# A hybrid layer on one core: the recurrent projection's products placed by unit, keys stored twice, two recurrent pools swapped

## The chip, the cores and the metric

One core of one Trainium2 chip runs the whole layer as one program. The metric is the device time of an execution in microseconds, given as the median of three runs. The engines are named as in the profile: PE (TensorE, matmuls), DVE (VectorE), ACT (ScalarE), POOL (GpSimd) and SP (SyncE, which here only issues DMAs). Sixteen DMA engines move data between HBM and the on-chip memory.

## The reference

One layer over 1024 latent and 256 context tokens, all in f32, 1024 channels:

```python
xn = modulate(rms_norm(x), sh1, sc1);  cn = modulate(rms_norm(h_ctx), csh1, csc1)
yg, xr, q, k, v, gr, gn = split_in(xn @ w_in[l] + b_in[l])     # seven parts of 1024
...                                                             # conv, gated linear recurrence, two directions
y_rnn = h_lat * jax.nn.gelu(yg)
q4 = axial_rope(q...);  k4 = axial_rope(k...)                   # 16 heads of 64
y_na = neighbourhood_attention(q4, k4, v4, kc4, vc4, na_rpb[l]) # window 8 x 16 plus 256 context keys
mix = jax.nn.sigmoid(gr) * (y_rnn @ w_proj_rnn[l]) + jax.nn.sigmoid(gn) * (y_na @ w_proj_na[l])
x = x + g1 * (mix @ w_out[l])
x = x + g2 * expert_choice_moe(xn2, w_router[l], w_exp_gate[l], w_exp_up[l], w_exp_down[l])  # 16 experts
return rms_norm(x) * final_norm
```

## The kernel before

Every f32 product is made of three products: an operand is split into a rounded high part and the rest (`hi`, `lo`), and `mm3` (lines 185 to 189) adds hi·hi, hi·lo and lo·hi in one PSUM tile. The stages follow each other: queries, keys and values (`stage_qkv`), the recurrent branch (`stage_lru`), attention (`stage_attn`), the merge of both branches, and the experts. No planner orders the instructions: each engine takes them in the order in which the Python code issues them, and waits in that order. SP's DMAs stand in one queue; each of them waits until the DMA that last used its semaphore, one of eight, has landed.

Weights come as chunks of 1 MB through `Stream`: `load` fetches a chunk into one of two ring tiles, `split` makes its `hi` on ACT (line 181) and its `lo` on DVE (line 98), and `take` hands it to PE, drops the one before and splits what has been loaded.

`stage_qkv` runs over four groups of four heads: query units, key units, value units, on PE some 80 us in all. A finished pair of units is rotated on DVE and POOL, then `out_parts` (line 477) splits it (`ohi` on ACT, `olo` on DVE, three buffers each) and stores both halves to HBM with line 484: four rows of 32 partitions by up to 512 tokens. Value results (`vo`, line 617, four buffers) are stored by line 618; in SP's queue these stores stand behind the group's key stores. `mod_rows` works on other weights (`wmr`, 16 MB through POOL's queue) beside this.

`stage_lru` weaves projections (PE) with a chain of elementwise work and scans (ACT, DVE, POOL) over eight blocks of 128 channels. It stores `y_rnn` as `d_yr` (line 752). Its tiles lie in the pools `tgp`, `lru2`, `lru3`, `lru1`, stacked in that order; the attention stage's pools come to lie over them, so a first load of the attention stage waits until whatever used those bytes is done.

`stage_attn` has 128 units n: a head and a strip of 128 queries. `attend` issues for unit n: `score` (products `sp`, then on DVE bias and row maximum, line 909), `turn` of unit n-3 (transposes `pt`, line 932, copied by ACT to `et`, line 934; `pt` has one buffer), `values` of units n-5 and n-6, `expo` (ACT), `scale` (DVE). `project` multiplies `y_rnn` by the weights `wpr`: two halves of 512 tokens, eight output blocks, eight groups (one `mm3` of three matmuls) per block. `weave` interleaves the two by a running cost that each yields:

```python
done += 0.55        # attend, after score; 0.5 after turn, 1.2 per two units for values
...
if k % 2 == 1:      # project: two groups at a time
    done += 0.8 * f
    yield done
```

The operand of these products, `y_rnn` as the tiles `x0h`, `x1h`, `x0l`, `x1l` of 1 MB each, is fetched by line 1012 for each half.

Of the kernel before, what the change touches and what calls it, by code (L numbers as in the profile page):

```python
# [12 lines left out]
F32 = mybir.dt.float32  # L13
F32R = mybir.dt.float32r
# [39 lines left out]

SKIP1, SKIP2 = 7, 7
IDLE = 1
A1, A2 = 3, 4

LRU_ORDER = ([("in", 0)] + [e for j in range(1, 6) for e in (("in", j), ("gate", j - 1))]
# [3 lines left out]
def raw(t, off, dims):  # L63
    return bass.AP(tensor=t.tensor, offset=t.offset + off, ap=dims)


class Stream:
# [33 lines left out]
    def split(self, most=9, defer=False, pieces=1):  # L101

        k = self.k
        most += self.nsplit
        while self.nsplit < min(self.nload, most) and self.chunks[self.nsplit][2] and self.pfree:
            i = self.nsplit
            slot = self.pfree.popleft()
            hi = slot[0].tile([128, 2048], F32R, name=slot[1] + "h", tag=slot[1] + "h")
            lo = slot[0].tile([128, 2048], F32R, name=slot[1] + "l", tag=slot[1] + "l")
            x, rslot = self.raws.pop(i)  # L110
            if pieces > 1:
                n = 2048 // pieces
# [12 lines left out]
            self.nsplit += 1  # L125

    def release(self):
        for i in self.held:
# [45 lines left out]
class Kernel:  # L174
# [28 lines left out]
    def run(self):  # L203
        tc, nc = self.tc, self.nc
        P = self.pools = {}
        left = []

        def open_(name, side="left", **kw):
            cm = tc.tile_pool(name=name, side=side, **kw)
            pool = cm.__enter__()  # L210
            return pool, cm

        self.open_ = open_
        self.const, c0 = open_("const", bufs=1)
        self.dram, c1 = open_("dram", bufs=1, space=DRAM)
        self.hip, c2 = open_("hip", bufs=1)
        self.ringp, c3 = open_("ringp", bufs=1)
        dr = lambda name, shape: self.dram.tile(shape, F32, name=name)
        self.d_q = self.dram.tile([16, 128, SEQ], F32R, name="d_q")
        self.d_k = self.dram.tile([16, 128, NT], F32R, name="d_k")  # L220
        self.d_v = dr("d_v", [10, 128, D])
        self.d_tgr = dr("d_tgr", [8, 128, SEQ])
        self.d_tgn = dr("d_tgn", [8, 128, SEQ])
        self.d_yr = [self.dram.tile([8, 128, SEQ], F32R, name="d_yr" + part) for part in "hl"]
        self.d_yn = [self.dram.tile([8, 128, SEQ], F32R, name="d_yn" + part) for part in "hl"]
        self.d_m1 = dr("d_m1", [8, 128, SEQ])
# [90 lines left out]
    def stage_qkv(self):  # L317
# [159 lines left out]
        def out_parts(dst, g, part, r, tok, n):  # L477
# [4 lines left out]
            width = dst.shape[2]  # L482
            for h, o in ((hi, 0), (lo, 64)):
                nc.sync.dma_start(raw(dst.bitcast(F32), (g * 512 + o + part * 32) * width + tok,
                                      [[128 * width, 4], [width, 32], [1, n]]), h[:, :n].bitcast(F32))

        def mod_rows():

# [166 lines left out]
    def stage_lru(self):  # L655
        nc, I, S = self.nc, self.I, self.S
        tgp, ctg = self.open_("tgp", side="right", bufs=1)
        p, cp = self.open_("lru2", side="right", bufs=1)
        last, clast = self.open_("lru3", side="right", bufs=1)
        first, cfirst = self.open_("lru1", side="right", bufs=1)  # L660
        ps, cps = self.open_("psl", bufs=1, space=PSUM)
        cneg, cpos = self.softplus_neg(first)
# [175 lines left out]
        weave(proj(), chain())  # L838
        cps.__exit__(None, None, None)
        cfirst.__exit__(None, None, None)  # L840
        clast.__exit__(None, None, None)
        cp.__exit__(None, None, None)
        ctg.__exit__(None, None, None)
        self.c_xn.__exit__(None, None, None)

# [2 lines left out]
    def stage_attn(self):  # L848
# [10 lines left out]
        def load_head(h):  # L859
# [5 lines left out]
            ks = []  # L865
            for part in range(2):
                t = pool.tile([128, NT], F32R, name=f"k{part}", tag=f"k{part}", bufs=2)
                for x in range(2):
                    nc.sync.dma_start(t[x * 64:(x + 1) * 64].bitcast(F32),
                                      self.d_k[h, part * 64:(part + 1) * 64].bitcast(F32))  # L870
                ks.append(t)
            L["h", h] = (q, ks)
        def load_v(h):
            if h < HEADS:
                v = (po if h % 4 else pb).tile([128, 10, 128], F32, name="v", tag="v")
# [83 lines left out]
                    nc.gpsimd.dma_start(d[pr, :, (s // 4) * 512:(s // 4 + 1) * 512].bitcast(F32), t.bitcast(F32))  # L959

        def attend():
            done = 0.0
            load_head(0)
            load_head(1)
            load_bias(0)
# [3 lines left out]
            for n in range(N + 6):  # L969
                if n < N:  # L970
# [17 lines left out]
                    done += 0.55  # L988
                if 0 <= n - 3 < N:
                    turn(n - 3)  # L990
                    done += 0.5
                if 0 <= n - 5 < N:
                    values(n - 5)
                    done += 1.2 * (n % 2 == 0)
                if n < N:
                    expo(n)
                yield done
                if 0 <= n - 1 < N:
                    scale(n - 1)

        def project():
            done = 5.0
            yield done
            f = 1.75

            def fetch(hf):

                ys = []
# [12 lines left out]
                    nc.sync.dma_start(tgs[hf, j], self.d_tgr[j, :, hf * 512:(hf + 1) * 512])  # L1021

            fetch_gate(0, 0)
            for hf in range(2):
                cs = slice(hf * 512, (hf + 1) * 512)
                yh, yl = fetch(hf)
                done += 12.0
                yield done
                for i in range(4):
                    hi, lo = S.take8()  # L1030
                    for x in range(2):
                        j = 2 * i + x
                        xs = slice(x * 128, (x + 1) * 128)
# [1 line left out]
                        fetch_gate(hf + (j + 1) // 8, (j + 1) % 8)  # L1035
                        pm = ps.tile([128, 512], F32, name="pr", tag="pr", bufs=1)
                        for k in range(8):
                            self.mm3(pm, hi[:, k, xs], lo[:, k, xs], yh[k // 4][:, k % 4], yl[k // 4][:, k % 4],
                                     k == 0, k == 7)
                            if k % 2 == 1:  # L1040
                                done += 0.8 * f
                                yield done
# [3 lines left out]
                        done += 2.0 * f  # L1046
                        yield done

        weave(attend(), project())
        cps.__exit__(None, None, None)  # L1050
        cpk.__exit__(None, None, None)
        cpo.__exit__(None, None, None)
# [920 lines left out]
```

## Time and profile before

| | |
|---|---|
| median of 3 runs | 2628.53 us (2625.5 to 2629.2) |
| profiled execution | 2631.97 us, its span on the core 2630.2 us |
| PE busy | 2490.4 us, 95% |
| DVE, ACT, POOL busy | 1888.0, 1535.5, 301.9 us |
| mean granted clock of PE | 0.978 of full speed |

The span is what lies between the first and the last instruction of the profiled execution. The queries, keys and values end at about 388 us, the recurrent stage at 844, attention at 1217; merge and experts take the rest. A busy share over the whole span hides that these stages have different limits, so windows of single stages are read below.

### The profile page before, as it was taken

Reading aid. Unit: us, or ns where it says so; the run is one execution under the profiler, and the core shown is the slowest. Engines: PE = TensorE matmul, PEld = TensorE weight load, DVE = VectorE, ACT = ScalarE, POOL = GpSimd, SP = SyncE. Lnnn points to the kernel's source line nnn. Section 1 sums busy time; section 2 is a strip of 40 time slices with the busy share of each in tenths; the row PEclk is TensorE's granted clock in tenths of the full one; section 3 lists DMA queues with packets and bytes.
Section 4 is the critical chain, followed back from the end, with each engine's and each line's share of the span. In section 5 each row is a group of like instructions: output and inputs, shape, how many; then the busy total and the mean of one; then the engine's idle time right before and its main releaser. Section 6 shows DMA issues by size and latency. Waiting matters only on the chain.

```text
span 2630.2 us, 34531 instructions
## 1 busy us (share of the span) xinstructions
PE 2490.4 (95%) x13401; PEld 2035.6 (77%) x13401; DVE 1888.0 (72%) x2300; ACT 1535.5 (58%) x1699; POOL 301.9 (11%) x269
## 2 busy tenths in 40 slices
PE   7999999999998799999997799999999999999996
PEld 4888888777886687787986577777777777777775
DVE  5675633655564566666466788888888898888888
ACT  5321125466655556565333577777777777777776
POOL 1321110121120000000120000000000000000001
PEclk9999999999999899999998899999999999999998
DMA  8354441122216959645875799999999999999985
GB/s 274 131 206 169 180 141 36 66 74 86 97 42 202 287 187 291 187 153 211 272 238 202 282 362 367 366 365 364 372 372 370 376 370 366 367 367 367 365 306 226
DMA packets 260148, 661.80 MB, mean 252 GB/s; under 512 B 18001, under 2 KB 35553, under 8 KB 250257
## 3 DMA queue, kind: packets, MB, share of 16 engines
q1 hardware_dynamic: 236768, 585.18, 62.8%
q0 software_dynamic: 15120, 62.21, 7.0%
q10 hardware_dynamic: 8096, 12.21, 1.5%
q8 instruction: 105, 1.72, 0.3%
q14 instruction: 59, 0.48, 0.1%
HBM read 585.02 MB, written 74.53 MB: 251 GB/s over the span
## 4 chain that ended last, share of the span: by engine, by line
PE 72%; DVE 10%; ACT 9%; DMA 5%; issue 3%; SPq 0%; ACTq 0%; POOLq 0%; DVEq 0%
PE pm L188 9%; PE pm L189 9%; PE pm L187 9%; PE po L187 3%; PE po L189 3%; PE po L188 3%; PE pv L949 2%; PE pp L187 2%; PE pp L188 2%; PE pp L189 2%; PE pt L932 2%; PE mm L187 2%; PE mm L189 2%; PE mm L188 2%; DVE w0l L98 2%
## 5 line engine op out<-in xcount | busy, mean ns | idle before, releaser
L98 DVE TENSOR_TENSOR w1l<-ring,w1h 128x2048 fp32r<-128x2048 f32 x150 | 343.3, 2288 | 72.5 <-ACT w1h L181 72.0
L98 DVE TENSOR_TENSOR w0l<-ring,w0h 128x2048 fp32r<-128x2048 f32 x123 | 281.8, 2291 | 81.6 <-ACT w0h L181 81.2
L181 ACT CAST w1h<-ring 128x2048 fp32r<-128x2048 f32 x150 | 286.2, 1908 | 70.8 <-PE pm L189 42.6
L181 ACT CAST w0h<-ring 128x2048 fp32r<-128x2048 f32 (+1 forms) x125 | 236.8, 1895 | 101.2 <-PE pm L189 45.2
L98 DVE TENSOR_TENSOR x0l<-ring,x0h 128x2048 fp32r<-128x2048 f32 x81 | 185.5, 2290 | 34.6 <-ACT x0h L181 34.4
L181 ACT CAST x0h<-ring 128x2048 fp32r<-128x2048 f32 x81 | 154.4, 1906 | 32.3 <-PE pm L189 16.3
L909 DVE CUSTOM_DVE_ANT_0 e<-sp,bias 128x640 f32<-128x640 f32 (+1 forms) x128 | 100.7, 787 | 83.1 <-PE sp L905 73.4
L188 PE MATMUL pm<-w0l,xeh 128*128 128x512 f32 x384 | 154.2, 402 | 2.8 <-DVE w0l L98 2.8
L187 PE MATMUL pm<-w0h,xeh 128*128 128x512 f32 x384 | 154.6, 403 | 1.7 <-ACT xeh L1681 1.7
L189 PE MATMUL pm<-w0h,xel 128*128 128x512 f32 x384 | 152.6, 397 | 0.0
L1760 POOL DMA_INDIRECT d_acc<-y,idx x15 | 50.5, 3366 | 873.0 <-DVE y L1759 873.0
L934 ACT COPY et<-pt 128x640 f32<-128x640 f32 (+1 forms) x128 | 84.7, 662 | 106.6 <-PE pt L932 104.9
L917 ACT ACTIVATE e<-e,mx 128x640 f32<-128x640 f32 (+1 forms) x128 | 103.0, 805 | 43.3 <-DVE mx L911 41.8
L187 PE MATMUL pm<-x0h,xeh 128*128 128x512 f32 x320 | 128.2, 401 | 0.0
L188 PE MATMUL pm<-w1l,xeh 128*128 128x512 f32 x320 | 128.1, 400 | 0.0
L187 PE MATMUL pm<-w1h,xeh 128*128 128x512 f32 x320 | 127.9, 400 | 0.0
L188 PE MATMUL pm<-x0l,xeh 128*128 128x512 f32 x320 | 126.8, 396 | 0.4 <-DVE x0l L98 0.4
L189 PE MATMUL pm<-w1h,xel 128*128 128x512 f32 x320 | 126.8, 396 | 0.0
L189 PE MATMUL pm<-x0h,xel 128*128 128x512 f32 x320 | 126.5, 395 | 0.0
L187 PE MATMUL pp<-xh,w1h 128*128 128x512 f32 (+1 forms) x304 | 116.3, 382 | 3.9 <-ACT tg L730 3.2
L188 PE MATMUL pp<-xl,w1h 128*128 128x512 f32 (+1 forms) x304 | 115.9, 381 | 0.0
L189 PE MATMUL pp<-xh,w1l 128*128 128x512 f32 (+1 forms) x304 | 115.7, 381 | 0.0
(458 smaller groups left out, 6894.0 us busy)
## 6 DMA issues: line engine op xcount, KB each, us to landing
ring<-w_exp_up SPq DMA_DIRECT2D x104, 1024.0 KB
ring<-w_exp_down SPq DMA_DIRECT2D x102, 1024.0 KB
ring<-w_exp_gate SPq DMA_DIRECT2D x100, 1024.0 KB
k<-d_k SPq DMA_DIRECT2D x64, 320.0 KB
wmr<-wm POOLq DMA_DIRECT2D x16, 1024.0 KB, 9.0
ring<-wrnn SPq DMA_DIRECT2D x16, 1024.0 KB
ring<-wqkv SPq DMA_DIRECT2D x12, 1024.0 KB
bias<-bias SPq DMA_DIRECT2D x16, 704.0 KB
```

The lines of the kernel that those rows point to most:

```text
L98: (engine or self.lo_engine).tensor_sub(lo, x, hi)
L181: self.nc.scalar.copy(hi, x)
L187: mm(out, wh, xh, start=first, stop=False)
L188: mm(out, wh, xl, start=False, stop=False)
L189: mm(out, wl, xh, start=False, stop=last)
L909: nc.vector.tensor_tensor_reduce(e[:, :w], sp[:, c0:c0 + w], b[:, b0:b0 + w], 1.0, -3.0e38, op0=ALU.add, op1=ALU.max, accum_out=mx[:, 0:1])
L917: nc.scalar.activation(e[:, :w], e[:, :w], AF.Exp, bias=mx[:, 1:2], accum_out=mx[:, 2:3])
L932: nc.tensor.transpose(pt[:, c * 128:(c + 1) * 128], e[:, c * 128:(c + 1) * 128], self.ident)
L934: nc.scalar.copy(et[:, :w], pt[:, :w])
L949: nc.tensor.matmul(pv[j * 64:(j + 1) * 64, (s % 4) * 128:(s % 4 + 1) * 128], v[:, t, j * 64:(j + 1) * 64], state[n - 1 + j][:, c * 128:(c ...
L1760: nc.gpsimd.indirect_dma_start(out=self.d_acc[:, :], out_offset=bass.IndirectOffsetOnAxis(ap=self.idx[:, e:e + 1], axis=0), in_=y[:, :], i ...
```

## The change

1. `out_parts` stores each half of a key twice, to rows 0 to 63 and 64 to 127 of a head's part, and `load_head` then reads 128 rows with one DMA where it read 64 rows twice.
2. `project` no longer yields a cost. It yields before each group, and `attend` yields after `score`: for unit n as many groups are issued there as the line through P0 and P1 (first half, 64 groups over 50 units from unit 11) and P2 and P3 (second half, 64 over 56 from unit 69) asks for. The fetch of the first half stands ahead of the unit loop's later loads; that of the second at the end of the first half.
3. `turn` comes four units behind (`BEHIND`) and not three, and after the products.
4. The next weight chunk is split in four pieces between products (`split_by`), not at once.
5. The pools `lru2` and `lru3` change places.

```diff
+BEHIND = 4
+P0, P1, P2, P3 = 11, 50, 69, 56
...
+    def split_by(self, n):
...
+        for c in range(0, 2048, 2048 // n):
+            cs = slice(c, c + 2048 // n)
+            self.k.hi_copy(hi[:, cs], x[:, cs])
+            self.lo_engine.tensor_sub(lo[:, cs], x[:, cs], hi[:, cs])
+            yield
...
-        self.d_k = self.dram.tile([16, 128, NT], F32R, name="d_k")
+        self.d_k = self.dram.tile([16, 2, 128, NT], F32R, name="d_k")
...
-            for h, o in ((hi, 0), (lo, 64)):
-                nc.sync.dma_start(raw(dst.bitcast(F32), (g * 512 + o + part * 32) * width + tok,
-                                      [[128 * width, 4], [width, 32], [1, n]]), h[:, :n].bitcast(F32))
+            step, at = (128, ((0,), (64,))) if dst is self.d_q else (256, ((0, 64), (128, 192)))
+            for h, os in zip((hi, lo), at):
+                for o in os:
+                    nc.sync.dma_start(raw(dst.bitcast(F32), (g * 4 * step + o + part * 32) * width + tok,
+                                          [[step * width, 4], [width, 32], [1, n]]), h[:, :n].bitcast(F32))
...
         tgp, ctg = self.open_("tgp", side="right", bufs=1)
+        last, clast = self.open_("lru3", side="right", bufs=1)
         p, cp = self.open_("lru2", side="right", bufs=1)
-        last, clast = self.open_("lru3", side="right", bufs=1)
...
-                for x in range(2):
-                    nc.sync.dma_start(t[x * 64:(x + 1) * 64].bitcast(F32),
-                                      self.d_k[h, part * 64:(part + 1) * 64].bitcast(F32))
+                nc.sync.dma_start(t.bitcast(F32), self.d_k[h, part].bitcast(F32))
...
-                if 0 <= n - 3 < N:
-                    turn(n - 3)
+                yield n
+                if 0 <= n - BEHIND < N:
+                    turn(n - BEHIND)
...
-                    hi, lo = S.take8()
+                    hi, lo = S.take8(most=0)
+                    more = S.split_by(4)
...
                         for k in range(8):
+                            yield
                             self.mm3(pm, hi[:, k, xs], lo[:, k, xs], yh[k // 4][:, k % 4], yl[k // 4][:, k % 4],
                                      k == 0, k == 7)
-                            if k % 2 == 1:
-                                done += 0.8 * f
-                                yield done
+                            if k % 4 == 2:
+                                next(more, None)
...
-        weave(attend(), project())
+        count, products = 0, project()
+        for n in attend():
+            if n == 0:
+                next(products)
+            due = min(64, (n - P0) * 64 // P1) + max(0, min(64, (n - P2) * 64 // P3))
+            while count < due:
+                next(products, None)
+                count += 1
+        for _ in products:
+            pass
```

SP's queue before, in the last group of the first stage: the key stores, the next weight chunk (`ring`), the value stores.

```order
L484 DMA d_k<-ohi 4x32x512
L484 DMA d_k<-olo 4x32x512
L484 DMA d_k<-ohi 4x32x512
L484 DMA d_k<-olo 4x32x512
L484 DMA d_k<-ohi 4x32x256
L484 DMA d_k<-olo 4x32x256
L484 DMA d_k<-ohi 4x32x256
L484 DMA d_k<-olo 4x32x256
L90 DMA ring_3098<-wrnn 128x2048
L618 DMA d_v<-vo 128x2x256 x5
```

The same place of SP's queue in the changed program, whose lines are numbered some 24 higher.

```order
L508 DMA d_k<-ohi 4x32x512 x2
L508 DMA d_k<-olo 4x32x512 x2
L508 DMA d_k<-ohi 4x32x512 x2
L508 DMA d_k<-olo 4x32x512 x2
L508 DMA d_k<-ohi 4x32x256 x2
L508 DMA d_k<-olo 4x32x256 x2
L508 DMA d_k<-ohi 4x32x256 x2
L508 DMA d_k<-olo 4x32x256 x2
L93 DMA ring_3146<-wrnn 128x2048
L642 DMA d_v<-vo 128x2x256 x5
```

Each key store has become two of the same shape, and weight chunk and value stores stand behind twice as many.

SP's queue before, at the start of attention, from the first pair's bias to the first two tiles of `y_rnn`.

```order
L882 DMA bias<-bias 128x1408 x2
L876 DMA v<-d_v 128x10x128
L864 DMA q<-d_q 128x1024
L869 DMA k_6452<-d_k 64x1280 x2
L869 DMA k_6455<-d_k 64x1280 x2
L882 DMA bias<-bias 128x1408 x2
L864 DMA q<-d_q 128x1024
L869 DMA k_6534<-d_k 64x1280 x2
L869 DMA k_6537<-d_k 64x1280 x2
L1021 DMA tgl<-d_tgr 128x512
L1012 DMA x0h<-d_yrh 128x4x512
L1012 DMA x1h<-d_yrh 128x4x512
```

The same place in the changed program.

```order
L905 DMA bias<-bias 128x1408 x2
L899 DMA v<-d_v 128x10x128
L1037 DMA tgl<-d_tgr 128x512
L1028 DMA x0h<-d_yrh 128x4x512
L1028 DMA x1h<-d_yrh 128x4x512
L1028 DMA x0l<-d_yrl 128x4x512
L1028 DMA x1l<-d_yrl 128x4x512
L93 DMA ring_6491<-wpr 128x2048
L1037 DMA tgl<-d_tgr 128x512
L888 DMA q<-d_q 128x1024
L892 DMA k_6511<-d_k 128x1280
L892 DMA k_6513<-d_k 128x1280
```

The tiles of `y_rnn` now stand ahead of the loads of the second pair of heads. The first bias load waited, before, for the last `hi` and `lo` stores of the recurrent stage and for its last gate stores; in the changed program for that `hi` store and for a subtraction before the `lo` store.

PE's order before, from the transposes issued with unit 13 over the first products to unit 14.

```order
L932 MATMUL pt<-ident,e 128x128 x5
L187 MATMUL pr<-x0h,w0h 128x512
L188 MATMUL pr<-x0l,w0h 128x512
L189 MATMUL pr<-x0h,w0l 128x512
L187 MATMUL pr<-x0h,w0h 128x512
L188 MATMUL pr<-x0l,w0h 128x512
L189 MATMUL pr<-x0h,w0l 128x512
L905 MATMUL sp<-k_6408,q 128x256
L905 MATMUL sp<-k_6411,q 128x256
L905 MATMUL sp<-k_6408,q 128x256
L905 MATMUL sp<-k_6411,q 128x256
L932 MATMUL pt<-ident,e 128x128 x5
```

The first products in the changed program, in unit 12.

```order
L928 MATMUL sp<-k_6456,q 128x256
L928 MATMUL sp<-k_6458,q 128x256
L928 MATMUL sp<-k_6456,q 128x384
L928 MATMUL sp<-k_6458,q 128x384
L208 MATMUL pr<-x0h,w0h 128x512
L209 MATMUL pr<-x0l,w0h 128x512
L210 MATMUL pr<-x0h,w0l 128x512
L955 MATMUL pt<-ident,e 128x128 x5
L972 MATMUL pv<-et,v 64x128 x10
```

The products moved from behind a unit's transposes to between its scores and the transposes, one group where two stood.

## Rows read from the trace of the kernel before

**Rows 1.** The page: busy time of PE, share of the span.
```profile
PE 2490.4 (95%) x13401; PEld 2035.6 (77%) x13401; DVE 1888.0 (72%) x2300; ACT 1535.5 (58%) x1699; POOL 301.9 (11%) x269
```
**Rows 2.** Stretches: length, busy us of each engine, PE's granted clock, DMA share, GB/s.
```profile
242.00:328.00 86.00, 86.00 (x510) 72.91 (x509) 57.83 (x91) 17.36 (x24) 15.12 (x14) 1.00 0.47 169
...
264.00:268.00 4.00, 4.00 (x19) 3.21 (x18) 3.88 (x6) 0.75 (x2) 0.97 (x1) 1.00 1.02 406
352.00:376.00 24.00, 24.00 (x196) 23.59 (x195) 6.93 (x9) 5.32 (x8) 3.09 (x2) 1.00 0.26 103
400.00:845.00 445.00, 433.12 (x1959) 353.74 (x1957) 248.42 (x178) 256.99 (x286) 72.68 (x65) 0.98 0.24 83
905.00:1150.00 245.00, 231.89 (x1857) 193.21 (x1858) 156.72 (x446) 141.62 (x269) 18.84 (x35) 1.00 0.73 225
1150.00:1217.00 67.00, 61.14 (x580) 50.71 (x579) 45.53 (x145) 45.67 (x90) 5.39 (x11) 1.00 0.40 131
```
**Rows 3.** The same for the start of attention, 845 to 905, with their sum.
```profile
850.00:860.00 10.00, 5.87 (x24) 4.89 (x24) 5.82 (x19) 4.25 (x10) 0.00 (x0) 0.53 1.07 305
...
880.00:890.00 10.00, 0.79 (x1) 0.28 (x1) 2.92 (x3) 1.94 (x3) 0.00 (x0) 0.50 0.98 348
...
sum 60.00, PE 38.95 PEld 31.68 DVE 29.66 ACT 27.04 POOL 1.63; mean PE 5.57 PEld 4.53 DVE 4.24 ACT 3.86 POOL 0.23
```
**Rows 4.** Who waited for the stores of line 484, 60 to 480: us, times.
```profile
  ACT ohi L479: 36.5, 8
  DVE olo L481: 34.8, 10
```
**Rows 5.** DMA from the first key store (86) to 392: total; issues, KB each.
```profile
DMA packets 19467, 51.60 MB, mean 169 GB/s; under 512 B 1075, under 2 KB 8243, under 8 KB 16067
...
d_k<-ohi SPq DMA_DIRECT2D x16, 256.0 KB
...
d_q<-ohi SPq DMA_DIRECT2D x14, 256.0 KB
...
d_k<-ohi SPq DMA_DIRECT2D x8, 128.0 KB
```
**Rows 6.** The chain that ended last, in the second group: start, us, what.
```profile
193.15 14.21 DMA d_k<-olo
...
210.08 0.60 DVE vo L617
```
**Rows 7.** Timeline, end of the third group and of the stage: start, us, instruction, idle before.
```profile
293.42 0.42 DVE L481 TENSOR_TENSOR olo<-qr,ohi 128x256 fp32r<-128x256 f32 x1 [4.71 <-DMA d_k<-olo]
...
314.63 0.69 DVE L617 TENSOR_TENSOR vo<-pv,bv 128x512 f32<-128x512 f32 x1 [3.83 <-DMA d_v<-vo]
...
389.05 0.36 PE L187 MATMUL pp<-xh,w0h 128*128 128x256 f32 x1 [0.88 <-DVE vo L617]
...
391.57 1.28 ACT L637 ACT_TABLE_LOAD   x1 [21.20 <-DMA d_v<-vo]
```
**Rows 8.** PE's timeline at its first two products: start, us, instruction, idle before.
```profile
884.96 0.79 PE L187 MATMUL pr<-x0h,w0h 128*128 128x512 f32 x1 [7.37 <-DMA x0h<-d_yrh]
890.35 0.79 PE L188 MATMUL pr<-x0l,w0h 128*128 128x512 f32 x1 [4.59 <-DMA x0l<-d_yrl]
```
**Rows 9.** Waits (DVE's, SP's; total, times, longest) and two of SP's issues, 845 to 870.
```profile
DVE e L909 <- DMA bias<-bias: 9.5, 2, 7.0
...
SPq L882 <- DMA d_yrl<-gel: 8.9, 1, 8.9
...
845.92 0.83 SPq L882 DMA_DIRECT2D bias<-bias  x2
...
868.80 0.38 SPq L1012 DMA_DIRECT2D x0h<-d_yrh  x1
```
**Rows 10.** What the transposes waited for from 905 to 1217: us, times.
```profile
  ACT et L934: 31.9, 63
  DVE e L924: 8.1, 9
```

More of the change, by code (lines that the diff above doesn't have):

```diff
@@ L125, in split @@
             self.nsplit += 1
+    def split_by(self, n):
+        i = self.nsplit
+        if i >= self.nload or not self.chunks[i][2] or not self.pfree:
+            return
+        self.nsplit += 1
+        slot = self.pfree.popleft()
+        hi = slot[0].tile([128, 2048], F32R, name=slot[1] + "h", tag=slot[1] + "h")
+        lo = slot[0].tile([128, 2048], F32R, name=slot[1] + "l", tag=slot[1] + "l")
+        x, rslot = self.raws.pop(i)
+        for c in range(0, 2048, 2048 // n):
[3 more added lines that the diff above has]
+            yield
+        self.free.append(rslot)
+        self.parts[i] = (hi, lo, slot)
     def release(self):
@@ L481, in out_parts @@
             nc.vector.tensor_sub(lo[:, :n], r[:, :n], hi[:, :n])
-            width = dst.shape[2]
-            for h, o in ((hi, 0), (lo, 64)):
-                nc.sync.dma_start(raw(dst.bitcast(F32), (g * 512 + o + part * 32) * width + tok,
-                                      [[128 * width, 4], [width, 32], [1, n]]), h[:, :n].bitcast(F32))
+            width = dst.shape[-1]
+            step, at = (128, ((0,), (64,))) if dst is self.d_q else (256, ((0, 64), (128, 192)))
[3 more added lines that the diff above has]
+                                          [[step * width, 4], [width, 32], [1, n]]), h[:, :n].bitcast(F32))
         def mod_rows():
@@ L840, in stage_lru @@
         cfirst.__exit__(None, None, None)
+        cp.__exit__(None, None, None)
         clast.__exit__(None, None, None)
-        cp.__exit__(None, None, None)
         ctg.__exit__(None, None, None)
@@ L961, in attend @@
         def attend():
-            done = 0.0
             load_head(0)
@@ L987, in attend @@
                     score(n)
-                    done += 0.55
-                if 0 <= n - 3 < N:
-                    turn(n - 3)
-                    done += 0.5
+                yield n
+                if 0 <= n - BEHIND < N:
+                    turn(n - BEHIND)
                 if 0 <= n - 5 < N:
                     values(n - 5)
-                    done += 1.2 * (n % 2 == 0)
                 if n < N:
                     expo(n)
-                yield done
                 if 0 <= n - 1 < N:
@@ L1001, in project @@
         def project():
-            done = 5.0
-            yield done
-            f = 1.75
             def fetch(hf):
@@ L1023, in project @@
             fetch_gate(0, 0)
+            yh, yl = fetch(0)
             for hf in range(2):
                 cs = slice(hf * 512, (hf + 1) * 512)
-                yh, yl = fetch(hf)
-                done += 12.0
-                yield done
                 for i in range(4):
-                    hi, lo = S.take8()
+                    hi, lo = S.take8(most=0)
+                    more = S.split_by(4)
                     for x in range(2):
@@ L1037, in project @@
                         for k in range(8):
+                            yield
                             self.mm3(pm, hi[:, k, xs], lo[:, k, xs], yh[k // 4][:, k % 4], yl[k // 4][:, k % 4],
                                      k == 0, k == 7)
-                            if k % 2 == 1:
-                                done += 0.8 * f
-                                yield done
+                            if k % 4 == 2:
+                                next(more, None)
                         m = po.tile([128, 512], F32, name="m1", tag="m1", bufs=2)
@@ L1045, in project @@
                         nc.gpsimd.dma_start(self.d_m1[j, :, cs], m)
-                        done += 2.0 * f
-                        yield done
-        weave(attend(), project())
+                    for _ in more:
+                        pass
+                if hf == 0:
+                    yh, yl = fetch(1)
+                yield
+        count, products = 0, project()
[7 more added lines that the diff above has]
+        for _ in products:
+            pass
         cps.__exit__(None, None, None)
```

## The prediction

> **What bounds the kernel now.** The busy table comes first: PE is busy for 95% of the span [rows 1], so a change is worth what it takes from or adds to PE's idle time. The stretches by stage show where that lies [rows 2]. In the query/key/value stage PE has no gap in the third group (86.00 of 86.00 us), in the recurrent stage it is busy 433.12 of 445. In attention it is busy 38.95 of the first 60 us [rows 3], then 231.89 of 245 and 61.14 of 67: 21.0, 13.1 and 5.9 us idle, 40 in all. [...]
>
> The DMA columns of the same rows tell of the stage whose stores are doubled. From 352 to 376 almost only key stores move: share 0.26, 103 GB/s. From 264 to 268 loads move as well: share 1.02, 406 GB/s. So a key store occupies some four of the sixteen engines, and several of them in the queue go no faster than one. ACT and DVE already wait 36.5 and 34.8 us for the stores' buffers [rows 4], and in the second group the chain that ended last runs for 14.21 us through a key store, to the `vo` behind it [rows 6].
>
> **The doubled key stores.** There are 16 of 256 KB and 8 of 128 KB for the high halves, as many for the low ones: 10.49 MB [rows 5]. At 103 GB/s [rows 2] that is 102 us of those four engines; the change adds 102 more. Is there room? The first key store is issued at about 86 us, and at 391.57 [rows 7] ACT enters the recurrent stage when the value stores have landed: 306 us. In them the core moves 51.60 MB [rows 5]. Key stores and 28 query stores (14 high and as many low, 256 KB each, 7.34 MB) are 17.8 MB on four engines, 173 us; the other 33.8 MB use all of them, at 406 GB/s 83 us. That is 256 of 306, 50 us free. The added 102 overrun this by 52 us, if not a microsecond of the four engines stays unused.
>
> How PE comes to feel it: of `ohi` and `olo` there are three buffers, so DVE stands at an `olo` until stores three steps back have landed (293.42, 4.71 us), and `vo` is queued behind it on DVE; PE has four PSUM tiles for values and then stops. The fifth `vo` needs the buffer of the first, whose store stands in SP's queue behind all key stores of its group (314.63, 3.83 us on `d_v`). The recurrent stage's first matmul waits for the last `vo` (389.05, 0.88 us), ACT's first work there for `d_v` (391.57) [rows 7]. With the last key stores 52 us later these all come 52 us later. I add 3 for gaps in which the four engines have nothing to do (each group's query stores start some us after the drain) and 3 for matmuls at the lower clock after PE's wait at the end (in [rows 3] two 10 us slices at half clock follow shorter waits): **+58**. The recurrent stage does not give it back: it has 12 us of PE idle in 445.
>
> Its bounds. From below 0, if a second store ran beside the first on other engines. If the earlier groups absorb theirs and only the last group's burst is longer, its twelve stores (2.62 MB, 26 us at 103 GB/s) take 26 more; counted from the drain at about 376 the first `vo` buffers come free at about 403 instead of 388: +14. From above +102, if the 50 free us can't be used. I take 58, since the row nearest to the question (352:376) shows a full queue that does not speed up.
>
> [...]
>
> **The start of attention.** The key loads as 128 rows move the same bytes with half the issues. While they are under way the DMA share is 1.07 and 0.98 [rows 3], so bytes and not issues bound them: 0. The move in SP's queue counts. Before, four biases of 0.72 MB, the values of 0.66, two heads of 1.84 each and a gate tile of 0.26 stood between the bias issue at 845.92 and `x0h`, issued at 868.80 [rows 9] and awaited by PE until 884.96 [rows 8]. Now it is two biases, the values and the gate tile, 2.4 MB; with the four `y_rnn` tiles (4.2 MB) 6.6 MB, at 305 GB/s [rows 3] 22 us, so by 868. PE stood at its first product from 877.6 (884.96 - 7.37), with unit 13 behind it; now the first comes in unit 12, some 3.5 us earlier, and the bias some 3, so at about 871. The waits of 7.37 and 4.59 us [rows 8] go: -12. The half clock behind them goes: -2. The first bias load waited 8.9 us for the last low store; now it waits for the high one, issued a little before: -3 of the 9.5 that DVE waited for bias [rows 9]. Late next are heads 2 and 3, now behind the tiles and a weight chunk: 6.4 MB after 868, 21 us at 305 GB/s, the last by 889, where unit 17 wants it at about 885: +4. Sum **-13**; bounds: -24 (the 21 us idle and the clock), and 0 if these heads cost as much as the tiles did.
>
> **The placement in the units.** After 905 PE idles 19 us [rows 2]. Transposes wait for ACT's copy out of the one `pt` buffer (31.9 us, weight loads counted beside matmuls, so more than PE's idle time) and for DVE's scaling (8.1) [rows 10]. A group of three matmuls between scores and transposes hides the rest of such a copy, one more unit of delay the scaling, and the last units, which had no products, get some. Not all goes: units 62 to 69 and those after 125 stay without products. I take a third of 19, **-7**, between -19 and +5 (transposes that stand later in the unit make ACT's copy and the values late). The chunks split in pieces add 24 instructions on DVE and 22 on ACT; DVE is busy 156.72 and ACT 141.62 of 245 [rows 2], which hides them. The second half's tiles (4.2 MB, 14 us at 305 GB/s) have those units 62 to 69 to land in, some 16 us: 0, at most +4. The pools' swap acts only through the first bias, counted above.
>
> **The sum.** 58 - 13 - 7 = +38. The profiled execution took 2631.97 us, 1.8 beyond its span of 2630.2, and 3.4 above the median of 2628.53. Its own time would become 2670; set on the median, 2628.5 + 38 = 2667.
>
> **The rivals.** *First: the copies are hidden and the change is faster.* The place is SP's queue in the first stage; it decides as soon as a second store does not wait for the first. Time: 2628.5 - 20 = 2608. For it: 50 us of the four engines are free, and the value and query parts of a group leave time between the bursts. Against: the full queue at 0.26, and a chain that already runs through these stores [rows 6]. 0.13. *Second: only the last burst is longer,* the others drain before the next query stores: +14 - 20, 2622; up to 2632 where attention wins half. For it: PE has four PSUM tiles for values and can run on while DVE stands. Against: the same waits. 0.11. *Third: heads 2 and 3 take the place of the tiles at the start of attention,* and products ahead of transposes win nothing, beside the slow first stage: 2628.5 + 58 + 5 = 2692, to 2700. For it: DMA at share 1.0 from 850 to 890. Against: unit 16 comes later than unit 13, where the tiles were missed. 0.10.
>
> **How the numbers follow.** Forecast 0.66; its own range goes from 2643 (+40 in the first stage, -25) to 2696 (+75, -8). Within 0.2%, about what this measurement can tell from no change, is 2623 to 2634. Faster: all of the first rival and half of the second, 0.19. Same: the rest of the second, 0.05. Slower: 0.76. The range from 2611 to 2697 leaves out most of the first rival and the end of the third.
>
> **What would show it.** Right: key bursts of about 52 us at share 0.26; DVE's and ACT's waits for these stores at over twice 71 us; PE idle in the value parts and before the first recurrent matmul, which comes near 447; after that the recurrent stage as long as before; no PE wait for `x0h`; PE busy above 95% from 905 shifted. Wrong: a share near 0.5 in a key burst, or a first recurrent matmul before 410, or idle time in attention as large as the 40 us of before.

## The result, and the profile after

The changed kernel takes 2689.71 us (median of 4 runs, 2686.58 to 2691.02), the kernel before 2628.86 beside it (4 runs, 2625.5 to 2631.93): a ratio of 1.0235, 95% interval 1.0221 to 1.025. It is 61 us slower. The forecast was 2667, slower by 38. The direction and the mechanism in the first stage hold; both large terms of the sum were too small, and since their signs differ the errors cancel in part.

The page of the changed kernel: busy time of the engines, and the chain that ended last, by engine and by line. In the chain, `DMA d_k<-olo` and `SPq L508` are the doubled key stores (line 508 is line 484 of before).

```profile
PE 2492.3 (93%) x13401; PEld 2041.3 (76%) x13401; DVE 1898.1 (71%) x2324; ACT 1535.5 (57%) x1723; POOL 303.2 (11%) x269
...
PE 63%; DVE 13%; DMA 9%; ACT 8%; issue 3%; SPq 3%; POOL 0%; ACTq 0%; POOLq 0%; DVEq 0%
PE pm L209 9%; PE pm L210 9%; PE pm L208 9%; DMA d_k<-olo 4%; PE po L208 3%; PE po L209 3%; PE po L210 3%; SPq L508 3%; PE pv L972 3%; PE sp L928 3%; PE pt L955 2%; PE pp L208 2%; PE pp L209 2%; PE pp L210 2%; PE mm L208 2%
```

PE did the same work in the same busy time as before (2492.3 against 2490.4 us) [rows 1]: nearly all of the 59 us by which the span is longer are time in which it stood. Where, the stretches by stage tell (length, busy us of PE, PEld, DVE, ACT, POOL; PE's granted clock, DMA share, GB/s):

```profile
242.00:328.00 86.00, 74.46 (x401) 62.45 (x402) 53.78 (x76) 15.37 (x19) 14.07 (x13) 0.90 0.50 175
440.00:460.00 20.00, 10.54 (x94) 10.35 (x92) 2.79 (x3) 2.61 (x3) 0.00 (x0) 0.85 0.26 102
490.00:943.00 453.00, 441.13 (x1987) 360.15 (x1985) 252.54 (x194) 258.74 (x289) 74.31 (x65) 0.98 0.23 82
943.00:1003.00 60.00, 55.99 (x453) 47.13 (x454) 44.24 (x137) 38.79 (x80) 3.25 (x6) 0.97 1.01 377
1003.00:1248.00 245.00, 242.56 (x2050) 205.49 (x2048) 177.75 (x526) 159.56 (x324) 20.01 (x37) 1.00 0.62 223
```

In the first stage the 86 us that PE had filled [rows 2] now hold 74.46. In the middle of a burst, the series of key stores of one group (440 to 460), only key stores move, at share 0.26 and 102 GB/s, as in [rows 2]. The recurrent stage has the same 12 us of idle time. In attention PE is busy 55.99 of the first 60 us, where it was 38.95 [rows 3], and 242.56 of the next 245, where it was 231.89 [rows 2].

Who waited for the stores of line 508, from 60 to 560 (us, times), and what PE waited for from 60 to 490 (us, times, longest):

```profile
  DVE olo L502: 108.2, 16
  ACT ohi L500: 96.3, 12
```

```profile
PE pv L208 <- DVE vo L641: 59.8, 4, 28.8
PE pp L208 <- DVE vo L641: 15.1, 1, 15.1
PE pt L545 <- DVE macc L535: 13.0, 2, 7.8
```

204.5 us of waits where [rows 4] had 71.3 (17 of them for query stores), and through `vo` they reach PE: 74.9 us. Another 13.0 come through `macc`, work of `mod_rows` that stands behind the waiting `olo` and `vo` in DVE's order; the kernel before and the one with keys stored once have no such wait. The last wait for `vo` stands ahead of the recurrent stage's first matmul, which came at 389.05 in [rows 7] (PE's timeline; the bracket is the idle time before):

```profile
483.45 0.55 PE L208 MATMUL pp<-xh,w0h 128*128 128x256 f32 x1 [15.12 <-DVE vo L641]
```

It comes 94.4 us later. Until then PE was idle for 94.6 of the 423.4 us from 60 on, before for 7.4 of 329. The scores of attention, first and last start, in the kernel before and in the changed one (line, engine, operation, count, shortest/median/longest ns, first to last):

```profile
L905 PE MATMUL sp<-k,q x512: 274/337/580, 846.1 to 1207.1; 128*128 128x256 f32 x107, 128*128 128x384 f32 x64
```

```profile
L928 PE MATMUL sp<-k,q x512: 274/337/583, 944.0 to 1264.3; 128*128 128x256 f32 x107, 128*128 128x384 f32 x64
```

Attention starts 97.9 us later and lasts 320.3 us instead of 361.0, 40.7 less. 97.9 - 40.7 = 57, of the span's 59. PE's waits in attention (943 to 1315), against [rows 8 to 10]; none is for `x0h`, `x0l` or the bias:

```profile
PE pt L955 <- ACT et L957: 4.7, 11, 0.8
PE sp L928 <- ACT tg L754: 1.5, 1, 1.5
PE mm L208 <- issue: 1.2, 1, 1.2
PE pr L208 <- DVE m L1059: 1.1, 1, 1.1
PE sp L928 <- DMA k<-d_k: 1.0, 1, 1.0
```

So two questions were open: why the stores cost 98 us and not 58, and where the 21 us in attention beyond the forecast 20 came from. In the experiments "score span" is the time from the first to the last start of `sp`.

### The profile page after: what moved, and what is told of

Same layout as the page of the kernel before. It is cut to its first block, busy times and chain, and to the rows that moved or that the text cites. A ratio compares the mean times of both kernels' runs of the same rounds, so it can differ in the third digit from the quotient of the medians.

```text
span 2689.2 us, 34474 instructions
## 1 busy us (share of the span) xinstructions
PE 2492.3 (93%) x13401; PEld 2041.3 (76%) x13401; DVE 1898.1 (71%) x2324; ACT 1535.5 (57%) x1723; POOL 303.2 (11%) x269
## 4 chain that ended last, share of the span: by engine, by line
PE 63%; DVE 13%; DMA 9%; ACT 8%; issue 3%; SPq 3%; POOL 0%; ACTq 0%; POOLq 0%; DVEq 0%
PE pm L209 9%; PE pm L210 9%; PE pm L208 9%; DMA d_k<-olo 4%; PE po L208 3%; PE po L209 3%; PE po L210 3%; SPq L508 3%; PE pv L972 3%; PE sp L928 3%; PE pt L955 2%; PE pp L208 2%; PE pp L209 2%; PE pp L210 2%; PE mm L208 2%
## 5 line engine op out<-in xcount | busy, mean ns | idle before, releaser
L101 DVE TENSOR_TENSOR w1l<-ring,w1h 128x2048 fp32r<-128x2048 f32 x146 | 334.1, 2289 | 59.0 <-ACT w1h L202 58.5
L202 ACT CAST w1h<-ring 128x2048 fp32r<-128x2048 f32 (+1 forms) x162 | 288.3, 1780 | 78.7 <-PE pm L210 42.6
L101 DVE TENSOR_TENSOR w0l<-ring,w0h 128x2048 fp32r<-128x2048 f32 x119 | 273.7, 2300 | 69.9 <-ACT w0h L202 68.5
L202 ACT CAST w0h<-ring 128x2048 fp32r<-128x2048 f32 (+2 forms) x137 | 238.9, 1745 | 128.9 <-DMA ring<-wqkv 67.4
L101 DVE TENSOR_TENSOR x0l<-ring,x0h 128x2048 fp32r<-128x2048 f32 x81 | 185.6, 2291 | 34.0 <-ACT x0h L202 31.7
L208 PE MATMUL pp<-xh,w0h 128*128 128x512 f32 (+1 forms) x272 | 108.3, 398 | 18.9 <-DVE vo L641 15.1
```

What stands on the lines that cost most here:

```text
L101: (engine or self.lo_engine).tensor_sub(lo, x, hi)
L202: self.nc.scalar.copy(hi, x)
L208: mm(out, wh, xh, start=first, stop=False)
```

## Experiments: the first part undone, and alone

**Keys stored once in the changed kernel.**

```diff
-        self.d_k = self.dram.tile([16, 2, 128, NT], F32R, name="d_k")
+        self.d_k = self.dram.tile([16, 128, NT], F32R, name="d_k")
...
-                nc.sync.dma_start(t.bitcast(F32), self.d_k[h, part].bitcast(F32))
+                for x in range(2):
+                    nc.sync.dma_start(t[x * 64:(x + 1) * 64].bitcast(F32),
+                                      self.d_k[h, part * 64:(part + 1) * 64].bitcast(F32))
```

(`out_parts` again stores each half once.)

> The changed kernel with its first part undone: keys stored once, and each key tile loaded by two transfers of 64 rows, as before the change; the units, the pools and the early fetch stay. Theory A (the second copies alone lengthen the first stage, by about 98 us; the rest of the change shortens the attention stage by about 39): 2629 - 39 = 2590 us, the last key store of the stage issued near 374 us, the first recurrent product near 389. Rival B (the early fetch, the split in pieces or the swapped pools delay the first stage or the recurrent one too): 2600 to 2650 us. Rival C (the attention stage won its 39 us because the doubled keys come with one transfer a tile): 2615 to 2630 us.

Measured: 2606.53 us (4 runs), ratio to before 0.9908 (0.9892 to 0.9925). None of the three fits whole. The first recurrent product comes at 390.2 and the first score at 847.2, both 1.1 us later than in the kernel before, so nearly all of the 98 us are the second copies' and rival B falls. But the score span is 333.9, so attention gained 27 and not 41: rival C holds for a third of the gain. The waits of PE at the start of attention say how (847 to 1209):

```profile
PE sp L927 <- DMA k<-d_k: 9.3, 2, 7.6
PE pt L954 <- ACT et L956: 3.9, 10, 0.8
```

With the 64-row loads the wait for `x0h` and `x0l` is gone, and 9.3 us for the keys of heads 2 and 3 have come in its place: the prediction's third rival, which the changed kernel escapes (1.0 us).

**The doubled keys alone, in the kernel before.** The same edit, the other way round.

> The kernel before with the first part of the change alone: keys stored twice, each key tile loaded by one transfer. Theory A: 2629 + 98 = 2727 us, attention as long as before. The sizing of the prediction (half of the extra store time finds room): 2629 + 58 = 2687 us. Rival C (the single transfer a tile shortens attention): 2690 to 2705 us.

Measured: 2714.33 us (4 runs), ratio 1.0319 (1.0302 to 1.0337). None of the three times was met: theory A had the first stage right, but the attention stage is shorter. The first score comes at 942.7 (+96.6) and the score span is 347.1 (-13.9). The two halves add up: 361.0 - 13.9 - 27.1 = 320.0, and the changed kernel has 320.3. Three of PE's waits in attention (943 to 1305):

```profile
PE pt L933 <- ACT et L935: 10.2, 32, 0.8
PE pt L933 <- DVE e L925: 8.1, 9, 1.8
...
PE pr L188 <- DMA x0l<-d_yrl: 0.3, 1, 0.3
```

With the quick loads alone, and the fetch of `y_rnn` at its old place, the 12 us that PE waited for `x0h` and `x0l` [rows 8] are down to 0.3. The transposes still wait for 18.3.

## Experiments: what makes a key store slow

**Doubled keys, stored by head.** Per key half four transfers of 32 rows, each writing both copies, instead of two of 4 x 32. The query stores stay as they are.

```diff
...
-                    nc.sync.dma_start(raw(dst.bitcast(F32), (g * 4 * step + o + part * 32) * width + tok,
-                                          [[step * width, 4], [width, 32], [1, n]]), h[:, :n].bitcast(F32))
...
+                    for y in range(4):
+                        nc.sync.dma_start(raw(dst.bitcast(F32), (g * 1024 + y * 256 + o + part * 32) * width + tok,
+                                              [[width, 32], [64 * width, 2], [1, n]]),
+                                          h[y * 32:(y + 1) * 32, None, :n].bitcast(F32).to_broadcast([32, 2, n]))
```

> The changed kernel, keys still stored twice with the same bytes, but each key part stored by four transfers, one for each head: 32 rows of the first copy and of the second (written from one source) instead of 4 heads x 32 rows. The outermost dimension of a transfer is then 32 and no longer 4. Theory A1 (a transfer whose outermost dimension is 4 runs on 4 of the 16 DMA engines): key bursts at a DMA share over 0.5 and over 200 GB/s instead of 0.27 and 103, waits of ACT and DVE for stores under 60 us instead of 204, and 2585 to 2605 us. Rival D (the stores are bound by their bytes, or by SyncE's issuing of them, whatever their shape): 2685 to 2720 us, bursts at 103 GB/s as before.

Measured: 2589.44 us (4 runs), ratio 0.9845 (0.9829 to 0.9861): 100 us under the changed kernel and 41 under the one before, with the same bytes stored. A stretch with the first burst (84 to 92, same columns as above), the first stage from the first key store on, and who waited for the key stores (nobody waits for the query stores here):

```profile
84.00:92.00 8.00, 8.00 (x36) 6.41 (x36) 3.42 (x6) 2.57 (x5) 2.47 (x2) 1.00 0.84 231
```

```profile
86.00:389.00 303.00, 301.25 (x1863) 261.68 (x1862) 186.11 (x290) 69.15 (x94) 57.89 (x58) 1.00 0.66 207
```

```profile
  ACT ohi L500: 26.2, 7
...
  DVE olo L502: 15.1, 6
```

Theory A1: share 0.84 in a burst, 41.3 us of waits, PE busy 301.25 of 303. At over three times the share of the old shape the rate is 231 GB/s, little more than twice its 102. The first recurrent product comes at 381.7, sooner than with single keys in the old shape (390.2). Rival D falls: neither the bytes nor twice as many issues (192 key stores instead of 96) cost anything that PE feels.

**Single keys and the queries by head** (the diff is against the kernel with keys stored once).

```diff
-                nc.sync.dma_start(raw(dst.bitcast(F32), (g * 512 + o + part * 32) * width + tok,
-                                      [[128 * width, 4], [width, 32], [1, n]]), h[:, :n].bitcast(F32))
+                for y in range(4):
+                    nc.sync.dma_start(raw(dst.bitcast(F32), ((g * 4 + y) * 128 + o + part * 32) * width + tok,
+                                          [[width, 32], [1, n]]), h[y * 32:(y + 1) * 32, :n].bitcast(F32))
```

> The changed kernel with keys stored once, and queries and keys both stored by four transfers, one for each head (32 rows each). Theory A1: waits of ACT and DVE for stores near 0 (71 us in the kernel before), first recurrent product at 365 to 385 us instead of 389, and 2565 to 2585 us. Rival D: as the kernel with keys stored once, 2590 us, or slower, up to 2610, since SyncE issues four times as many.

Measured: 2598.39 us (4 runs), ratio 0.9878 (0.9862 to 0.9895), 8 under the single keys in the old shape. The first recurrent product comes at 381.5, as theory A1 had it, and ACT and DVE wait 19 us for the stores; but the time missed its 2565 to 2585. PE fills the first stage whether keys go once or, stored by head, twice (381.5 and 381.7), so little is left to win there, and attention pays for the 64-row loads (score span 333.8).

**Single keys by two heads.** The rival that smaller transfers are just quicker needed a smaller transfer with a smaller outermost dimension: 2 heads x 32 rows (the diff is again against the kernel with keys stored once).

```diff
-            for h, o in ((hi, 0), (lo, 64)):
-                nc.sync.dma_start(raw(dst.bitcast(F32), (g * 512 + o + part * 32) * width + tok,
-                                      [[128 * width, 4], [width, 32], [1, n]]), h[:, :n].bitcast(F32))
+            m = 4 if dst is self.d_q else 2
+            for h, o in ((hi, 0), (lo, 64)):
+                for y in range(0, 4, m):
+                    nc.sync.dma_start(raw(dst.bitcast(F32), (g * 512 + y * 128 + o + part * 32) * width + tok,
+                                          [[128 * width, m], [width, 32], [1, n]]),
+                                      h[y * 32:(y + m) * 32, :n].bitcast(F32))
```

> The changed kernel with keys stored once (2606.5 us), each key half by two transfers of 2 heads x 32 rows instead of one of 4 heads x 32 rows: the same bytes, rows and row lengths, twice the transfers. Theory A1 (the outermost dimension sets how many of the 16 DMA engines work on a transfer, here 2): bursts at a share near 0.14 and some 50 GB/s, as long as those of the doubled stores, and 2690 to 2715 us. Rival S (smaller transfers are quicker whatever their shape, which is what the stores by head won): 2587 to 2607 us.

Measured: 2699.68 us (5 runs), ratio 1.0268 (1.0254 to 1.0282). A burst from 440 to 460, where again only key stores move, and the stores of line 507 (ns from issue to issue: shortest/median/longest, first and last start):

```profile
440.00:460.00 20.00, 11.66 (x99) 11.45 (x98) 2.41 (x3) 2.61 (x3) 0.00 (x0) 0.84 0.13 51
```

```profile
L507 SPq DMA_DIRECT2D d_k<-ohi x48: 484/2375/7311, 84.9 to 468.5; - x48
L507 SPq DMA_DIRECT2D d_k<-olo x48: 477/2382/7767, 86.0 to 471.2; - x48
```

Half the share and half the rate of the 4 x 32 store (0.26, 102). 128 KB in this shape hold SP's queue as long (2.38 us) as 256 KB in the other (2.39 to 2.47 us in the last burst of the kernel before), and the whole first stage is again as late as with doubled keys. Theory A1. Bytes, rows and row length are those of the single keys; what differs is how many heads go into a transfer. With one head in a transfer, 32 rows outermost, the stores are quick (231 GB/s), with two (51) they are slower than with four (102): so in these runs it is the outermost dimension and not the size that makes them slow. The share was 0.13 with 2, 0.26 with 4 and 0.84 with 32; of sixteen engines these are, as an estimate, some 2, 4 and 13. Which engines they were, no row here shows.

**Two buffers instead of three** for `ohi` and `olo`, in the changed kernel.

```diff
-            hi = p.tile([128, 512], F32R, name="ohi", tag="ohi", bufs=3)
+            hi = p.tile([128, 512], F32R, name="ohi", tag="ohi", bufs=2)
...
-            lo = p.tile([128, 512], F32R, name="olo", tag="olo", bufs=3)
+            lo = p.tile([128, 512], F32R, name="olo", tag="olo", bufs=2)
```

> The changed kernel (keys stored twice, 4 heads x 32 rows a transfer), with two buffers instead of three for the halves that wait to be stored. It asks why the extra store time found no room in the rest of a group. Theory Q (a burst of key stores is longer than the key products, and only what the buffers hold of it can run on beside the value products): one pair of halves less, 4 stores of 2.4 us in each of 4 groups, so 15 to 45 us slower than 2690 us. Rival R (the stores keep their queue busy all through a group, so that buffers change nothing): 2685 to 2697 us.

Measured: 2702.51 us (5 runs), ratio 1.0279 (1.0265 to 1.0293): 13 slower than the changed kernel, between the two expectations. PE's wait for `vo` in the value products grew from 59.8 to 81.7 us, and that ahead of the recurrent stage fell from 15.1 to 4.7; the first recurrent product came at 495.8, 12 later. The buffers carry a part of the burst past the key products, but less than their four stores' time per group.

## Experiments: where attention won

All on the doubled keys by head (2589.4 us, score span 320.5). Their first stage is the same, and yet the first recurrent product comes between 381.2 and 388.1 in the profiled executions. So a few microseconds between two times say little here, and the score span, which leaves the first stage out, says more.

**The key tile by two loads of 64 rows**, each from its own stored copy.

```diff
-                nc.sync.dma_start(t.bitcast(F32), self.d_k[h, part].bitcast(F32))
+                for x in range(2):
+                    xs = slice(x * 64, (x + 1) * 64)
+                    nc.sync.dma_start(t[xs].bitcast(F32), self.d_k[h, part, xs].bitcast(F32))
```

> As the kernel with doubled keys stored by head (2589.4 us), but each key tile of 128 rows loaded by two transfers of 64 rows, from the two stored copies. It asks why the attention stage was 13 to 14 us shorter with the keys stored twice. Theory E (a load of 64 rows moves fewer bytes in a microsecond than one of 128): 2600 to 2604 us, about 9 us of TensorE's waits for k at heads 2 and 3, the first 30 us of attention near 345 GB/s. Rival F (what cost time was that the same rows were read twice): 2587 to 2592 us, no such wait, near 395 GB/s.

Measured: 2600.31 us (4 runs), ratio 0.9884 (0.9869 to 0.9899), score span 334.6, PE's wait for `k` 9.5 us. Theory E. The first two stretches of 30 us of attention with 64-row loads in this kernel, and the same two with 128-row loads in the doubled keys by head (columns as above):

```profile
839.00:869.00 30.00, 26.29 (x196) 21.94 (x197) 21.04 (x69) 18.96 (x39) 1.09 (x2) 0.83 1.04 343
869.00:899.00 30.00, 20.52 (x156) 17.15 (x154) 12.58 (x38) 11.07 (x24) 0.54 (x1) 0.77 1.00 263
```

```profile
839.00:869.00 30.00, 27.03 (x228) 22.07 (x229) 24.37 (x79) 20.89 (x43) 1.09 (x2) 1.00 1.04 397
869.00:899.00 30.00, 29.04 (x234) 24.66 (x233) 20.66 (x60) 18.47 (x38) 2.17 (x4) 1.00 0.95 349
```

The DMA engines are busy nearly all the time in both (share 0.95 to 1.04), and move 343 and 263 GB/s with the one, 397 and 349 with the other. Two transfers, one on each half of the rows, did not come up to one over all 128. What makes a 64-row load slow, no row here shows: these transfers are also half as large, and no run loaded 128 rows by smaller transfers, so the two are not told apart.

**The pools in their old order.** `lru2` is opened before `lru3` and closed after it again.

> As the kernel with doubled keys stored by head (2589.4 us), with the two recurrent pools in the order of the kernel before. Theory G (the order only sets when the first bias lands, 5 to 6 us later, and the first products of TensorE cover a part of it): 2590 to 2596 us. Rival H (all of it is covered): 2587 to 2591 us, and the first exponents start at the same place.

Measured: 2594.6 us (4 runs), ratio 0.9862 (0.9847 to 0.9877), score span 325.2, with one wait of PE's of 6.3 us, for the `mx` that stands behind the first bias; in the base such waits add up to 1.4. Theory G: some 5 us. The times' intervals overlap with those of the base; the score span's 4.7 us bear it out.

**The first fetch of `y` later.**

```diff
             fetch_gate(0, 0)
+            yield
             yh, yl = fetch(0)
...
             if n == 0:
                 next(products)
+            if n == 5:
+                next(products)
```

> As the kernel with doubled keys stored by head (2589.4 us), with the first fetch of y (x0h to x1l) and the first weights' split placed at the fifth step of attention instead of the first, about where the kernel before had them. Theory I (the early fetch took away the waits for x0h and x0l, 12 us in the kernel before): 2596 to 2602 us with those waits back. Rival J (the waits were due to the key loads ahead of the fetch, which are quicker now; the late fetch is in time): 2587 to 2592 us, waits for x0h and x0l under 1 us.

Measured: 2594.43 us (4 runs), ratio 0.9868 (0.9853 to 0.9883), score span 324.0, one wait of 2.7 us for `x0l`. Between the two: nearly all of the 12 us of [rows 8] had been due to the slow key loads ahead of the fetch, as the run with the doubled keys alone shows too (0.3 us). Where the loads are quick, the early fetch is worth the wait of 2.7 us. The granted clock was 0.91 in the first 60 us of attention where it was 1.00 in the base, and more than 2.7 can't be told from that.

**Transposes three units behind instead of four** (`BEHIND = 3`).

> As the kernel with doubled keys stored by head (2589.4 us), with the transposes three units behind the scores instead of four, as in the kernel before; the recurrent products stay placed between scores and transposes. Theory K (the fourth unit took away the transposes' waits, 16 us in the kernel before and 5 now): 2597 to 2603 us, transposes waiting 13 to 18 us. Rival L (products between scores and transposes are cover enough): 2587 to 2592 us, waits of transposes under 8 us.

Measured: 2588.4 us (5 runs), ratio 0.984 (0.9827 to 0.9854), transposes waiting 4.7 us. Rival L: the fourth unit does nothing here.

**Weights split whole.**

```diff
-                    hi, lo = S.take8(most=0)
-                    more = S.split_by(4)
+                    hi, lo = S.take8()
+                    more = iter(())
```

> As the kernel with doubled keys stored by head (2589.4 us), with each projection weight split by one copy and one subtraction of 2048 columns, as in the kernel before, instead of four pieces of 512 among the products. Theory M (the whole split held VectorE and ScalarE, and the transposes waited for their e and et behind it): 2594 to 2600 us, transposes waiting 10 us or more. Rival N (with products placed between scores and transposes nobody waits for the split): 2587 to 2592 us.

Measured: 2592.13 us (4 runs), ratio 0.986 (0.9845 to 0.9875), transposes waiting 5.3 us: rival N, just above its upper end. The score span is 324.6, but the granted clock was 0.91 in its first 60 us here too; nothing separates this from no effect.

**Products behind the transposes and values** instead of between scores and transposes (the `yield n` moved behind `expo(n)`).

> As the kernel with doubled keys stored by head (2589.4 us), with the recurrent products placed behind the unit's transposes and values instead of between its scores and transposes; number and pace of the products as they are. Theory O (it is this place that took away the transposes' waits, 16 us before and 5 now): 2596 to 2603 us, transposes waiting 12 to 18 us. Rival P (it is the even pace, one or two groups to a unit instead of whole tiles): 2587 to 2593 us, transposes waiting under 8 us.

Measured: 2591.48 us (4 runs), ratio 0.9854 (0.9838 to 0.9871), score span 320.7, transposes waiting 5.3 us: rival P. It isn't the place within the unit.

Of the 27 us that attention won without the key loads, the pools have about 5 and the early fetch about 3. Undone one at a time, the place, the fourth unit and the pieces change nothing that can be told from no change; undone together they were not run, so one may stand in for another. What is left, some 19 us, belongs to what all these kernels keep, above all the count that spreads the products evenly over the units, in place of the weave by due costs. The waits say where most of it lies: PE's transposes waited 18.3 us with the doubled keys alone, 4.7 in the changed kernel and 3.7 to 5.3 in every run of this section. That the count is the cause is by elimination; the old weave with all else new was not run, so this part stays argued.

## Why the prediction was right and wrong

**The doubled stores: mechanism right, size wrong.** Share 0.26 in the burst, waits of DVE and ACT more than twice 71 us, `vo` behind them, PE idle ahead of the recurrent stage: each as forecast. The first recurrent product was to come near 447 and came at 483.45. The step that failed is the one that set 256 of 306 us of work against the stage as a whole and let 50 free us take half of the copies. SP's timeline shows why they don't (start, time, issues): the first and last key stores of the second group and the query store of the third, in the kernel before and in the changed one.

```profile
182.03 0.52 SPq L484 DMA_DIRECT2D d_k<-ohi  x1
...
211.31 1.30 SPq L484 DMA_DIRECT2D d_k<-olo  x1
...
242.12 0.52 SPq L484 DMA_DIRECT2D d_q<-ohi  x1
```

```profile
202.75 1.38 SPq L508 DMA_DIRECT2D d_k<-ohi  x2
...
262.22 2.84 SPq L508 DMA_DIRECT2D d_k<-olo  x2
...
288.68 0.51 SPq L508 DMA_DIRECT2D d_q<-ohi  x1
```

The burst grew from 30.6 us (182.03 to 212.6) to 62.3 (202.75 to 265.1). From its end to the next query store, while values and then queries are computed, the engines of the stores, some four of sixteen by the share of 0.26, have no key to store: this gap shrank only from 29.5 to 23.6, since PE could run ahead no further than `vo` allowed. Per group 31.7 - 5.9 = 26 us are added, against 24 in the mean (94.4 in four groups). The free time lay in a part of the group that the copies can't reach; the upper bound of 102 was nearly the answer, and the 50 us should have been looked up part by part. The two-buffer run shows the buffers as a part of what limits it.

**The first stage's delay reaches the end:** right. The recurrent stage gave nothing back. From its first product to the first score it took 460.6 us instead of 457.1, with a granted clock of 0.88 in its first 20 us where it had been 1.00: close to the +3 set aside for the lower clock after PE's wait. So 94.4 became 97.9.

**The start of attention: right in what goes, wrong in why.** "Bytes and not issues bound them: 0" was the failed step: at much the same share (0.95 to 1.04) the 128-row loads move more bytes (397 and 349 GB/s against 343 and 263), which alone is worth 13.9 us in the kernel before. The share of busy engines was read as a rate. The -12 for the tiles of `y_rnn` went as forecast, but not by their place in SP's queue: with the loads alone 0.3 us of it were left, and with the place alone 9.3 us of waits for heads 2 and 3 came instead. The +4 for these heads, and the third rival that rests on them, exist only with 64-row loads (9.3 and 9.5 us). The pools' part, -3, was about 5.

**The placement: -7 was too small.** The failed step is "a third of 19". It is about 19 us by elimination, as much as the bound: the 13.1 us that PE idled in the 245 us behind the start [rows 2] are 2.4 now. A third of the idle time was taken where nearly all of it went. That the pieces cost nothing was right.

**The total:** first stage +98 for +58, attention -41 for -20. Neither lies in the range that the forecast gave it (+40 to +75, and -8 to -25); the one was 40 too low and the other 21 too weak, and that the sum still came within 23 us is luck, since these errors have opposite signs. The first rival's time (2608) was reached by another way than it said: not by hidden copies in this shape, but by stores in another.

## What to carry to other kernels

Before a store is doubled or moved, look at the DMA share in a stretch where it runs alone: at 0.26 it was the shape of the transfer and not its bytes that cost, and cutting it so that 32 rows are outermost was worth 100 us here, more than the whole change. Free time of a queue counts only where the producer's buffers let the work get to it (here the burst grew by 31.7 us and the gap shrank by 5.9), so set bursts against gaps part by part and not over a stage. Loads that span all 128 rows were worth a second copy in memory here, once that copy was stored in a good shape (2589.4 us, against 2598.4 with one copy).

## What was unexpected of the hardware

A DMA share of 1.00 stood for 263 GB/s in one stretch, and one of 0.95 for 349 in the same stretch of a kernel that differs in its key loads alone: busy engines can be slow ones. A store with 2 outermost moved 51 GB/s, with 4 102, and 128 KB in the first took as long as 256 KB in the second (some 2.4 us). A store that reads one source row and writes it to two places went without a loss that PE would notice (busy for 301.25 of 303 us in the first stage).
